# Seven of nine conditioning vectors summed on VectorE instead of made on TensorE

## The chip, the core and the metric

The kernel runs on one core of a Trainium2 chip. A core has five engines with one instruction queue each: PE (TensorE, matrix products into PSUM), DVE (VectorE), ACT (ScalarE), POOL (GpSimd) and SP, whose queue here issues nearly all DMAs. Every queue is worked off in order. The metric is the device time of the whole program in microseconds (us), the median of several runs.

## The reference

One layer of a diffusion backbone, in float32, on 1024 latent tokens and 128 context tokens: a feed-forward block with half weight, a token mixer (attention beside a gated recurrence), a second feed-forward block, a final norm. What matters here is how the conditioning enters:

```
mod_p = (silu(c_ctx) @ w_ada + b_ada).reshape(9, 1024)   # context tokens
mod_s = (silu(c)     @ w_ada + b_ada).reshape(9, 1024)   # latent tokens
x = x + 0.5 * m[2] * swiglu(modulate(x, g[0], m[0], m[1]), w1, w3, w2)
x = x + m[5] * token_mixer(modulate(x, g[1], m[3], m[4]), ...)
x = x + 0.5 * m[8] * swiglu(modulate(x, g[2], m[6], m[7]), w1', w3', w2')
# modulate(x, g, shift, scale) = rmsnorm(x, g) * (1 + scale) + shift
```

So there are nine vectors of 1024 numbers, each for two conditions, m[0] to m[8], and each is a product of a 1024-vector with a 1024x1024 slice of `w_ada` (4 MB). A gate m[2] is first needed when the first feed-forward block's results are added to x, m[3] and m[4] at the first norm behind that block, m[5] behind the mixer, m[6] and m[7] at the norm after that, m[8] at the end.

## The kernel before, in words

Activations are kept with features on the 128 partitions and all 1152 tokens along the free dimension, so x is eight tiles of 128x1152. Every float32 product is made of three TensorE products of split operands (high x high, low x high, high x low, `mm3`), which is why nearly every operand is first split: ACT writes the high part, POOL or DVE subtracts it to get the low part.

A feed-forward block (`ffn_fast`, called with l=0 and l=1) has three parts:

- **Plain blocks.** The first `PLAIN` = 4 (l=0) or 3 (l=1) of 22 hidden blocks, eight products of 128x288 per hidden block.
- **Half products.** The other 18 (19) hidden blocks in a scheme that makes seven products of half depth instead of eight (`fast_block`, L1484; its weights come from `fast_ops`, L1449). Per hidden block there are seven steps n; in each step PE makes one half product for two column pairs, each of 12 matmuls of 128x288 into one PSUM bank. DVE reads the bank out into `et` (L1507 to L1521), makes the low part of the next weights (`wo`, L1479), and POOL makes sums of weight pieces (L1474).
- **The way down.** The hidden activations come back from DRAM two hidden blocks at a time (`hr`, L1573), are split by ACT and POOL (L1579, L1580), as are their weights (L238, L239). `down_group` (L451) then goes over eight feature blocks m and three column chunks; one chunk (a tick) is six matmuls into a PSUM bank called `dn` (three of them), and DVE adds the bank, times the gate, to x (L442). Nine such groups per block for l=0, then `down_last`.

**The nine vectors** are made by `ada_pe` (L247): eight row blocks of 512 KB are loaded, and for each PE makes four small float32 matmuls with the SiLU of both conditions as 32-column weights; ACT, two transposes and one DVE instruction finish a vector, `ada_end` scales it. m[1] and m[0] are made at the start, m[2] beside the first plain blocks (L1533), and m[3] to m[8] on the way down of l=0 (L1616): `self.bg` is advanced on every fourth tick.

**What sets the order.** The program's order of calls is a priority. A scheduler places each engine's instructions in its queue beforehand, and an instruction of lower priority is pulled ahead where the scheduler finds the engine free, so the calls of a background generator such as `bg` don't stand where they are called. Buffers come from rings (`half` six, `wide` eight, `slim` four, `tt` 25 tiles); a tile that is reused waits for its last reader.

Of the kernel before, what the change touches and what calls it, by code (L numbers as in the profile page):

```python
# [9 lines left out]
F32 = mybir.dt.float32  # L10
F32R = mybir.dt.float32r
BF16 = mybir.dt.bfloat16
U8 = mybir.dt.uint8
AF = mybir.ActivationFunctionType
ALU = mybir.AluOpType
# [4 lines left out]
P = 128  # L20
D = 1024
KT = D // P
# [40 lines left out]
def rows(w, m):  # L63

    return w[m // 4][:, ts(m % 4, P)] if isinstance(w, list) else w[:, 0, ts(m, P)]
# [12 lines left out]
def weave(gens):  # L78
    gens = list(gens)
    while gens:  # L80
        for g in list(gens):
            try:
                yield next(g)
            except StopIteration:
                gens.remove(g)


class Trunk:
# [158 lines left out]
    def ada_pe(self, m, buf):  # L247
# [26 lines left out]
        )  # L274
        self.ada_end(m)

    def ada_end(self, m):
        nc = self.nc
        if m in (2, 8):
            nc.vector.tensor_scalar(self.modt[:, m], self.modt[:, m], 0.5, None, ALU.mult)  # L280
        if m % 3 == 1:
            nc.vector.scalar_tensor_tensor(
                self.gs[:, m // 3],
                self.modt[:, m],
                1.0,
                self.ng[:, m // 3].unsqueeze(2).to_broadcast([P, KT, 2]),
                ALU.add,
                ALU.mult,
            )
# [161 lines left out]
    def down_group(self, w2, fs, hs, gm, ws=None):  # L451
        ws = ws or [self.load_w(w2[f], 1, D) for f in fs]
        for m in range(KT):
            for c in self.chunks:
                self.down([(rows(wh, m), rows(wl, m)) for wh, wl in ws], hs, gm, c, m)
                self.ticks += 1
                if self.ticks % 4 == 0:
                    next(self.bg, None)

    def down_last(self, w2, fs, hs, gm, nxt):  # L460
# [1064 lines left out]
    def ffn_fast(self, l, gm, nxt):  # L1525

        nc = self.nc
        w2 = self.a["w2"][l]
        plain = PLAIN[l]
        self.hs = self.dp.tile([NF, P, T], F32, name=f"hs{l}")  # L1530
        self.puts, self.ticks = [], 0
        sums, ops, made = iter(()), iter(()), []
        steps = iter(()) if l else weave([self.whole(), self.ada_pe(2, lambda k: self.wide("wada"))])  # L1533
        for f in range(plain):
            ws = self.pre[f] if l == 0 and f < 2 else [self.load_w(self.a["w13"][l, f, j], KT, P) for j in range(2)]
            if f == 2 - l:
                for _ in steps if l == 0 else self.tail:
                    pass
                sums = self.sums()
            if f == plain - 1:  # L1540
                ops = self.fast_ops(l, range(plain, NF))
            n = 0

            def after():
                nonlocal n
                if l and f == 0:
                    next(self.tail, None)
                elif f < 2 - l:
                    next(steps, None)
                else:  # L1550
                    next(sums, None)
                if f == plain - 1 and n > 7 and n % 2:
                    made.append(next(ops))
                n += 1

            self.plain_block(l, f, ws, after)
        for _ in sums:
            pass
        made = [w for w in made if w]
        self.B = None  # L1560
        pend, ws, raws = [], [], []
        tile = partial(self.tt, F32) if l == 0 else self.wide
        split = partial(self.wide, dt=F32R) if l == 0 else partial(self.tt, F32R)
        spare = partial(self.tt, F32R) if l == 0 else partial(self.wide, dt=F32R)

        def load_x(k):
            t = self.tt(F32, f"x{k}")
            nc.sync.dma_start(t[:, :T], self.xs[k] if l else self.a["xT"][k])
            return t

        def load_h(f):
            raw = tile("hr")[:, :T]
            nc.sync.dma_start(raw, self.hs[f])  # L1573
            return f, raw

        def split_h(f, raw):
            new = partial(self.tt, F32R) if f in (16, 17) else split
            hh, hl = new(name="hh")[:, :T], new(name="hl")[:, :T]
            nc.scalar.copy(hh, raw)  # L1579
            nc.gpsimd.tensor_sub(hl, raw, hh)  # L1580
            return f, (hh, hl)

        def load_w2(f):
            return self.load_w(w2[f], 1, D, home=spare if f % 2 else None)

        for f in range(plain, NF):
            blocks = [self.fast_block(f, r) for r in range(2)]
            for g in blocks:
                next(g)
            for n in range(7):  # L1590
                if len(made) < 6:
                    w = next(ops, None)
                    if w:
                        made.append(w)
                w = made.pop(0)
                for t in self.puts:
                    self.put(*t)
                self.puts = []
                for g in blocks:
                    g.send(w)  # L1600
                if f == NF - 1:
                    if n == 2:
                        raws = [load_h(0), load_h(1)]
                    elif n == 3:
                        ws.append(load_w2(0))
                        pend.append(split_h(*raws[0]))
                    elif n == 4:
                        pend.append(split_h(*raws[1]))
                    elif n == 5:
                        ws.append(load_w2(1))  # L1610
                        self.x = [load_x(0), load_x(1)]
        for t in self.puts:
            self.put(*t)
        self.x += [load_x(k) for k in range(2, KT)]
        if l == 0:
            self.bg = chain(*[self.ada_pe(m, lambda k: self.tt(F32, "wada")) for m in range(3, 9)])  # L1616
        for f in range(2, NF):
            pend.append(split_h(*load_h(f)))
            if f % 2 and f < NF - 1:
                fs, hs = zip(*pend[:2])  # L1620
                self.down_group(w2, fs, hs, gm, ws or [load_w2(v) for v in fs])
                pend, ws = pend[2:], None
        for _ in self.bg:
            pass
        fs, hs = zip(*pend)
        self.down_last(w2, fs, hs, gm, nxt)


def layout(inp):
    import numpy as np  # L1630

    f = lambda n: np.asarray(inp[n])
# [4 lines left out]
    a = {}  # L1637
# [14 lines left out]
        1,  # L1652
    )
    a["w_ada"] = f("w_ada")[0]
    a["w13"] = np.stack(
        [np.stack([tiles(f(f"ffn{l}_w1")[0]), tiles(f(f"ffn{l}_w3")[0])], 1) for l in (1, 2)]
    )
# [2 lines left out]
    o = np.cumsum([0, 384, 256, 32, 512, 512, 512, 512, 512, 1024, 1024])  # L1660
    qc, kvc, kr, hq, hff, hfb, hi, hgt, ga, gr = [wi[:, o[i] : o[i + 1]] for i in range(10)]
    sl = lambda w, i, n: w[:, i * n : (i + 1) * n]
    ws = []
# [83 lines left out]
```

## Time and profile before

| | us |
|---|---|
| median of 3 runs | 3035.35 (3032.83 to 3035.94) |
| the profiled execution | 3036.94 |
| its span | 3035.2 |
| PE busy | 2928.8 (96%) |
| DVE busy | 1897.1 (63%) |
| POOL busy | 1031.6 (34%) |

The span is the time from the first to the last instruction of the profiled execution. In time, the start and plain blocks of l=0 end at about 160 us, its half products run to about 562, its way down to about 860, the mixer follows, and the second feed-forward block with its own half products and way down ends the program. PE is busy in nearly every slice; DVE is busy for a good half of most.

### The profile page before, as it was taken

The numbers are of one execution on the slowest core, as the hardware profiler recorded it, in microseconds if no ns is written. First come the engines' busy times: TensorE is split into PE (matmuls) and PEld (weight loads), VectorE is DVE, ScalarE is ACT, GpSimd is POOL, SyncE is SP. The second block draws the span as 40 slices with busy tenths as digits, with TensorE's granted clock in tenths as the row PEclk, the third lists the DMA queues.
The fourth block names the chain that finished last, engine by engine and source line by source line (L and its number), as shares of the span: only waits on it lengthen the run. The fifth ranks groups of instructions, "written<-read, shape, count | busy, mean of one in ns | idle before, by whom it ended". The sixth has DMA issues, their size and how long they took to land. (4 is left out here: it accounts for less than half of the span.)

```text
span 3035.2 us, 49626 instructions
## 1 busy us (share of the span) xinstructions
PE 2928.8 (96%) x18960; PEld 2747.1 (91%) x18960; DVE 1897.1 (63%) x3751; ACT 1234.9 (41%) x2370; POOL 1031.6 (34%) x831
## 2 busy tenths in 40 slices
PE   7999999999999999999999999989999999999998
PEld 5899999988888988888998778779989999999997
DVE  7665455455568777787636677765674555546665
ACT  5432232211165464645434677741262222332113
POOL 3122222434233333332325444533242222226324
PEclk9999999999999999999999999999999999999999
DMA  6632222754221111111110000143352222226211
GB/s 244 228 100 77 72 74 73 299 188 174 84 94 46 43 43 47 38 45 45 59 62 20 11 17 21 52 146 104 101 187 74 74 73 77 77 95 220 89 44 63
DMA packets 141678, 279.25 MB, mean 92 GB/s; under 512 B 18112, under 2 KB 82560, under 8 KB 141440
## 3 DMA queue, kind: packets, MB, share of 16 engines
q1 hardware_dynamic: 141296, 275.75, 26.8%
q8 instruction: 150, 2.46, 0.3%
q14 instruction: 88, 0.72, 0.1%
q10 hardware_dynamic: 144, 0.33, 0.0%
HBM read 212.49 MB, written 63.52 MB: 91 GB/s over the span
## 5 line engine op out<-in xcount | busy, mean ns | idle before, releaser
L442 DVE SCALAR_TENSOR_TENSOR x<-dn,modt,x 128x256 f32<-128x256 f32 (+4 forms) x728 | 353.5, 506 | 237.1 <-PE dn L415 236.5
L1503 PE MATMUL b<-xo,wo 128*128 128x288 f32 x3552 | 484.3, 295 | 0.0
L1503 PEld LDWEIGHTS b<-xo,wo 128*128 128x128 f32 x3552 | 476.2, 188 | 0.0
L413 PE MATMUL mm<-xh,wh 128*128 128x384 f32 (+1 forms) x1008 | 361.9, 359 | 5.4 <-DVE q L610 3.2
L1503 PE MATMUL b<-bh,wo 128*128 128x288 f32 x1776 | 365.7, 295 | 0.0
L239 POOL TENSOR_TENSOR wl<-raw,wh 128x1024 fp32r<-128x1024 f32 (+1 forms) x106 | 235.8, 2226 | 380.7 <-ACT wh L238 378.1
L415 PE MATMUL mm<-xh,wl 128*128 128x384 f32 (+1 forms) x1008 | 342.6, 340 | 2.0 <-POOL wl L239 1.8
L414 PE MATMUL mm<-xl,wh 128*128 128x384 f32 (+1 forms) x1008 | 342.2, 339 | 0.0
L1503 PEld LDWEIGHTS b<-bh,wo 128*128 128x128 f32 x1776 | 288.7, 188 | 0.0
L1503 PE MATMUL b<-bl,wo 128*128 128x288 f32 x888 | 261.4, 294 | 0.0
L1478 ACT CAST wo<-raw 128x512 fp32r<-128x512 f32 x185 | 114.8, 621 | 256.3 <-PE b L1503 155.9
L238 ACT CAST wh<-raw 128x1024 fp32r<-128x1024 f32 (+1 forms) x108 | 104.3, 967 | 254.2 <-PE dn L414 142.3
L413 PEld LDWEIGHTS mm<-xh,wh 128*128 128x128 f32 (+1 forms) x1008 | 190.9, 189 | 15.3 <-DVE q L610 4.0
L413 PE MATMUL dn<-hh,wh 128*128 128x384 f32 (+2 forms) x576 | 201.2, 349 | 2.4 <-DVE x L442 1.2
L1479 DVE TENSOR_TENSOR wo<-raw,wo 128x512 fp32r<-128x512 f32 x185 | 128.7, 697 | 117.0 <-ACT wo L1478 116.4
L415 PE MATMUL dn<-hh,wl 128*128 128x384 f32 (+2 forms) x576 | 194.6, 338 | 1.0 <-POOL wl L239 1.0
L414 PE MATMUL dn<-hl,wh 128*128 128x384 f32 (+2 forms) x576 | 194.0, 337 | 0.0
L415 PEld LDWEIGHTS mm<-xh,wl 128*128 128x128 f32 (+1 forms) x1008 | 190.6, 189 | 3.6 <-POOL wl L239 2.1
L414 PEld LDWEIGHTS mm<-xl,wh 128*128 128x128 f32 (+1 forms) x1008 | 191.0, 189 | 1.7 <-issue 0.4
L1580 POOL TENSOR_TENSOR hl<-hr,hh 128x1152 fp32r<-128x1152 f32 x44 | 117.8, 2686 | 193.2 <-PE dn L414 87.6
L1237 POOL TENSOR_TENSOR ehl<-e,ehl 128x512 fp32r<-128x512 f32 x93 | 122.4, 1321 | 142.0 <-ACT ehl L1235 79.0
L1503 PEld LDWEIGHTS b<-bl,wo 128*128 128x128 f32 x888 | 167.3, 188 | 0.0
(379 smaller groups left out, 6996.3 us busy)
## 6 DMA issues: line engine op xcount, KB each, us to landing
raw<-in_w SPq DMA_DIRECT2D x148, 256.0 KB, 3.0
wada<-in_w_ada SPq DMA_DIRECT2D x72, 512.0 KB, 5.8
raw<-in_w SPq DMA_DIRECT2D x58, 512.0 KB, 3.8
hr<-hs SPq DMA_DIRECT2D x44, 576.0 KB, 4.8
hs<-et SPq DMA_DIRECT2D x148, 144.0 KB, 1.7
raw<-in_w_in SPq DMA_DIRECT2D x41, 512.0 KB, 3.6
hb<-hd SPq DMA_DIRECT2D x44, 288.0 KB, 3.3
x<-in_xT SPq DMA_DIRECT2D x16, 576.0 KB, 8.7
```

What stands on the lines that cost most here:

```text
L238: pin(self.nc.scalar.copy(wh, raw))
L239: pin((eng or self.nc.gpsimd).tensor_sub(wl, raw, wh))
L413: nc.tensor.matmul(ps, wh, xh, start=start and i == 0, stop=False)
L414: nc.tensor.matmul(ps, wh, xl, start=False, stop=False)
L415: nc.tensor.matmul(ps, wl, xh, start=False, stop=stop and i == n - 1)
L442: nc.vector.scalar_tensor_tensor(self.x[m][:, a:b], ps[:, a - lo : b - lo], self.modt[:, gm, m, s : s + 1], self.x[m][:, a:b], ALU.mult, A ...
L1237: eng.tensor_sub(el, e, eh)
L1478: nc.scalar.copy(wh, src[i])
L1479: nc.vector.tensor_sub(wl, src[i], wh)
L1503: nc.tensor.matmul(ps, w[:, k], x[:, k, :QW], start=first, stop=last, skip_group_check=home != i)
L1580: nc.gpsimd.tensor_sub(hl, raw, hh)
```

## The change

Only m[0] and m[1] are still made by `ada_pe`. A new generator, `ada_sum`, makes the others on DVE. `w_ada` is given a second time, transposed, so that output features lie on partitions and the 1024 inputs along the free dimension, in two halves of 512. A unit is one vector, one output block of 128 and one half: its weights (256 KB) are loaded into one half of a `wada` tile, so two loads can be there at a time, and two DVE instructions, one per condition, multiply them with the SiLU of the condition (broadcast to all partitions, `cb`) and write the sum over the 512 into one column of `adac`; the product itself goes to `junk`. A vector is 16 units. m[2] to m[5] (64 units) go beside the half products of l=0, m[6] and m[7] (32 units) on the way down of l=0, m[8] (16 units) beside the half products of l=1. On the way down the background is advanced on every third tick now.

```diff
+    def ada_sum(self, ms, cb, w2, small, fine=False):
+        nc, a = self.nc, self.a
+        HD = D // 2
+        acc = small("adac")[:, : 32 * len(ms)].rearrange("p (m h k s) -> p m h k s", m=len(ms), h=2, k=KT)
+        junk = small("junk").bitcast(BF16)[:, :HD]
+        w2 = w2("wada")
+        ws = [w2[:, :HD], w2[:, HD : 2 * HD]]
+        units = [(h, i, k) for h in range(2) for i in range(len(ms)) for k in range(KT)]
+        def load(n):
+            h, i, k = units[n]
+            nc.sync.dma_start(ws[n % 2], a["w_aT"][ms[i] - 2, k, :, ts(h, HD)])
...
+        for n, (h, i, k) in enumerate(units):
+            if not i and not k:
+                cs = [cb("cb")[:, :HD] for _ in range(2)]
...
+                for s in range(2):
+                    nc.scalar.activation(cs[s], cs[s], AF.Silu)
+                yield
+            if n + 1 < len(units):
+                load(n + 1)
+            for s in range(2):
+                o = acc[:, i, h, k, s : s + 1]
+                nc.vector.scalar_tensor_tensor(junk, ws[n % 2], 1.0, cs[s], ALU.mult, ALU.mult, accum_out=o)
+                if fine and not s:
+                    yield
+            if h and k == KT - 1:
+                nc.vector.tensor_add(acc[:, i, 0], acc[:, i, 0], acc[:, i, 1])
+                b = self.bada[:, ms[i]].unsqueeze(2).to_broadcast([P, KT, 2])
+                nc.vector.tensor_tensor(self.modt[:, ms[i]], acc[:, i, 0], b, ALU.add)
+                self.ada_end(ms[i])
+            yield
...
-                if self.ticks % 4 == 0:
+                if self.ticks % 3 == 0:
                     next(self.bg, None)
...
-        steps = iter(()) if l else weave([self.whole(), self.ada_pe(2, lambda k: self.wide("wada"))])
+        steps = iter(()) if l else self.whole()
...
+        ada = self.ada_sum((8,) if l else (2, 3, 4, 5), self.half, partial(self.tt, F32), self.slim)
...
+                if (n in (1, 4)) if l else (7 * f + n) % 3:
+                    next(ada, None)
...
-            self.bg = chain(*[self.ada_pe(m, lambda k: self.tt(F32, "wada")) for m in range(3, 9)])
+            new = partial(self.tt, F32)
+            self.bg = self.ada_sum((6, 7), new, new, self.slim, True)
```

How the queues change is seen at three places. First DVE in the half products of l=0, from the second product of a hidden block on, before: the bank reads into `et` and the low weight parts `wo`.

```order
L1507 TENSOR_TENSOR et<-b_2295,et 128x288
L1507 TENSOR_TENSOR et<-b_2309,et 128x288
L1479 TENSOR_TENSOR wo<-raw,wo 128x512
L1509 TENSOR_TENSOR et<-b_2326,et 128x288
L1509 TENSOR_TENSOR et<-b_2340,et 128x288
L1479 TENSOR_TENSOR wo<-ws,wo 128x512
L1511 TENSOR_TENSOR et<-b_2361,et 128x288
```

The same place in the changed kernel (lines are 39 higher), where `junk,adac` is a sum of a unit:

```order
L1546 TENSOR_TENSOR et<-b_2029,et 128x288
L306 SCALAR_TENSOR_TENSOR junk,adac<-wada,cb 128x512 x2
L1546 TENSOR_TENSOR et<-b_2043,et 128x288
L1518 TENSOR_TENSOR wo<-raw,wo 128x512
L306 SCALAR_TENSOR_TENSOR junk,adac<-wada,cb 128x512
L1548 TENSOR_TENSOR et<-b_2060,et 128x288
L306 SCALAR_TENSOR_TENSOR junk,adac<-wada,cb 128x512
L1548 TENSOR_TENSOR et<-b_2074,et 128x288
L1518 TENSOR_TENSOR wo<-ws,wo 128x512
L306 SCALAR_TENSOR_TENSOR junk,adac<-wada,cb 128x512
L1550 TENSOR_TENSOR et<-b_2098,et 128x288
L306 SCALAR_TENSOR_TENSOR junk,adac<-wada,cb 128x512 x2
```

The scheduler pulled the sums together: 17 stand in one hidden block, nearly twice what the calls would spread, so each half of the 64 units fills about four hidden blocks without a gap, and the others have none.

Then DVE on the way down of l=0, two feature blocks m, before:

```order
L442 SCALAR_TENSOR_TENSOR x_5986<-dn,modt,x_5986 128x256
L442 SCALAR_TENSOR_TENSOR x_5986<-dn,modt,x_5986 128x128
L442 SCALAR_TENSOR_TENSOR x_5986<-dn,modt,x_5986 128x384 x2
L442 SCALAR_TENSOR_TENSOR x_5988<-dn,modt,x_5988 128x256
L442 SCALAR_TENSOR_TENSOR x_5988<-dn,modt,x_5988 128x128
L442 SCALAR_TENSOR_TENSOR x_5988<-dn,modt,x_5988 128x384 x2
```

and in the changed kernel:

```order
L481 SCALAR_TENSOR_TENSOR x_6147<-dn,modt,x_6147 128x256
L481 SCALAR_TENSOR_TENSOR x_6147<-dn,modt,x_6147 128x128
L306 SCALAR_TENSOR_TENSOR junk,adac<-wada,cb 128x512
L481 SCALAR_TENSOR_TENSOR x_6147<-dn,modt,x_6147 128x384
L306 SCALAR_TENSOR_TENSOR junk,adac<-wada,cb 128x512
L481 SCALAR_TENSOR_TENSOR x_6147<-dn,modt,x_6147 128x384
L481 SCALAR_TENSOR_TENSOR x_6149<-dn,modt,x_6149 128x256
```

Two sums stand in each feature block, through 33 feature blocks, a little over four of the nine groups.

Last SP's queue at the start of the way down in the changed kernel (before, `wada` loads of 128x1024 stood there in sixes):

```order
L1613 DMA hr<-hs_631 128x1152 x2
L289 DMA wada<-in_w_aT 128x512
L244 DMA raw<-in_w 128x1024
L289 DMA wada<-in_w_aT 128x512
L244 DMA raw<-in_w 128x1024
L1613 DMA hr<-hs_631 128x1152
L289 DMA wada<-in_w_aT 128x512
```

Each unit's load now stands between loads of activations (`hr`) and weights (`raw`), which wait for buffers.

## Rows read from the trace of the kernel before

**Rows 1.** The page's first part: busy us, share, instructions.
```profile
PE 2928.8 (96%) x18960; PEld 2747.1 (91%) x18960; DVE 1897.1 (63%) x3751; ACT 1234.9 (41%) x2370; POOL 1031.6 (34%) x831
```

**Rows 2.** Stretches: start:end, length, each engine's busy us, clock, DMA share, GB/s.
```profile
80.00:160.00 80.00, 76.75 (x585) 73.26 (x585) 56.54 (x120) 37.42 (x73) 12.05 (x6) 0.98 0.67 220
200.00:240.00 40.00, 40.00 (x304) 40.00 (x303) 20.69 (x39) 11.58 (x23) 10.13 (x8) 1.00 0.22 73
560.00:600.00 40.00, 39.20 (x254) 34.20 (x253) 22.61 (x46) 7.41 (x8) 15.42 (x7) 1.00 1.00 390
600.00:640.00 40.00, 40.00 (x260) 34.66 (x259) 21.08 (x44) 6.38 (x7) 16.18 (x7) 1.00 0.66 243
```

**Rows 3.** PE's waits between 80 and 160 us: total us, times, longest.
```profile
PE adap L254 <- DMA wada<-in_w_ada: 2.8, 2, 1.4
PE adat L268 <- ACT adar L265: 0.5, 1, 0.5
```

**Rows 4.** PE in time on the way down: start, us, instruction, count.
```profile
642.57 0.33 PE L414 MATMUL dn<-hl,wxh 128*128 128x384 f32 x1
642.74 0.34 PE L415 MATMUL dn<-hh,wxl 128*128 128x384 f32 x1
643.01 0.64 PE L254 MATMUL adap<-wada,sc 128*32 128x256 f32 x8
643.58 0.45 PE L413 MATMUL dn<-hh,wh 128*128 128x384 f32 x1
643.87 0.33 PE L414 MATMUL dn<-hl,wh 128*128 128x384 f32 x1
...
647.70 0.34 PE L415 MATMUL dn<-hh,wxl 128*128 128x384 f32 x1
647.88 0.38 PE L268 MATMUL adat<-ident,adar 128*128 128x128 f32 x2
648.01 0.42 PE L413 MATMUL dn<-hh,wh 128*128 128x384 f32 x1
648.27 0.33 PE L414 MATMUL dn<-hl,wh 128*128 128x384 f32 x1
```

**Rows 5.** DVE in time at the start of the way down.
```profile
565.33 1.79 DVE L442 SCALAR_TENSOR_TENSOR x<-dn,modt,x 128x256 f32<-128x256 f32 x4
```

**Rows 6.** DVE instructions by form: out<-in, count, busy us, mean ns.
```profile
L317 DVE SCALAR_TENSOR_TENSOR rs<-rt,rs 128x512 f32<-128x512 f32 x1 | 0.7, 677 | 0.0
L316 DVE SCALAR_TENSOR_TENSOR rt<-rt,rs 128x512 f32<-128x512 f32 x1 | 1.2, 1249 | 0.0
L442 DVE SCALAR_TENSOR_TENSOR x<-dn,modt,x 128x384 f32<-128x384 f32 x304 | 187.6, 618 | 133.1 <-PE dn L415 133.0
L442 DVE SCALAR_TENSOR_TENSOR x<-dn,modt,x 128x256 f32<-128x256 f32 x152 | 73.6, 484 | 78.1 <-PE dn L415 78.0
L442 DVE SCALAR_TENSOR_TENSOR x<-dn,modt,x 128x128 f32<-128x128 f32 x176 | 60.3, 343 | 0.0
```

**Rows 7.** ACT's instructions of line 1252, the only sum with its elementwise result.
```profile
L1252 ACT ACTIVATION_READ_ACCUMULATOR pc<-sps,nm x8: 189/198/203, 1713.5 to 1997.9; 128x1 f32 x8
```

**Rows 8.** DVE and POOL in time where the second half products end.
```profile
2730.08 5.33 POOL L1580 TENSOR_TENSOR hl<-hr,hh 128x1152 fp32r<-128x1152 f32 x2
2732.32 0.46 DVE L1515 TENSOR_TENSOR et<-b,et 128x288 f32<-128x288 f32 x1 [4.31 <-PE b L1503]
2732.88 2.84 DVE L1516 TENSOR_TENSOR et<-et 128x288 f32<-128x288 f32 x1
2735.36 2.61 POOL L239 TENSOR_TENSOR wl<-raw,wh 128x1024 fp32r<-128x1024 f32 x1
2735.64 0.45 DVE L1515 TENSOR_TENSOR et<-b,et 128x288 f32<-128x288 f32 x1
2736.19 2.10 DVE L1516 TENSOR_TENSOR et<-et 128x288 f32<-128x288 f32 x1
```

**Rows 9.** POOL by form, the first row between 200 and 500 us, the others 600:760.
```profile
L1474 POOL TENSOR_TENSOR raw<-raw,ws 128x512 f32<-128x512 f32 x14 | 18.1, 1289 | 126.4 <-issue 126.4
...
L1580 POOL TENSOR_TENSOR hl<-hr,hh 128x1152 fp32r<-128x1152 f32 x13 | 34.8, 2681 | 39.2 <-PE adap L254 26.7 <-PE dn L414 6.4 <-ACT hh L1579 6.1
L239 POOL TENSOR_TENSOR wl<-raw,wh 128x1024 fp32r<-128x1024 f32 x6 | 14.4, 2399 | 0.0
```

**Rows 10.** Loads: KB each, median us to landing, the page's first, then 535 to 610 us.
```profile
raw<-in_w SPq DMA_DIRECT2D x148, 256.0 KB, 3.0
...
wada<-in_w_ada SPq DMA_DIRECT2D x18, 512.0 KB, 10.3
hr<-hs SPq DMA_DIRECT2D x10, 576.0 KB, 8.6
```

More of the change, by code (lines that the diff above doesn't have):

```diff
@@ L275, in ada_pe @@
         self.ada_end(m)
+    def ada_sum(self, ms, cb, w2, small, fine=False):
[9 more added lines that the diff above has]
+            nc.sync.dma_start(ws[n % 2], a["w_aT"][ms[i] - 2, k, :, ts(h, HD)])
+        cs = None
+        for n, (h, i, k) in enumerate(units):
+            if not i and not k:
+                cs = [cb("cb")[:, :HD] for _ in range(2)]
+                for s in range(2):
+                    nc.sync.dma_start(cs[s], a["cr"][s : s + 1, ts(h, HD)].to_broadcast([P, HD]))
+                if not n:
+                    load(0)
+                for s in range(2):
[3 more added lines that the diff above has]
+                load(n + 1)
+            for s in range(2):
+                o = acc[:, i, h, k, s : s + 1]
[8 more added lines that the diff above has]
+            yield
     def ada_end(self, m):
@@ L1611, in ffn_fast @@
                         self.x = [load_x(0), load_x(1)]
+        assert next(ada, 1) == 1
         for t in self.puts:
@@ L1654, in layout @@
     a["w_ada"] = f("w_ada")[0]
+    a["w_aT"] = f("w_ada")[0][:, 2 * D :].T.reshape(7, KT, P, D)
+    a["cr"] = np.concatenate([f("c"), f("c_ctx")[None]])
     a["w13"] = np.stack(
```

## Prediction

> **What bounds the kernel now.** I read the page first, then the busy time by stretches, then the time lines of the two stages that the change touches. PE is busy for 96% of the span [rows 1], and in the half products and on the way down for practically all of it, at full clock [rows 2]. So every microsecond of PE work that goes is a microsecond of the span, as long as nothing else comes last. DVE is the engine that takes the work over. It is busy for 20.69 of 40 us in the half products and 21.08 of 40 on the way down [rows 2], so the reader is to ask not whether it has room on average, but whether it has room where the scheduler has put the new sums.
>
> **What goes.** On the way down, one row block of a vector sits between two ticks. The matmul starting at 642.74 and the second after it, at 643.87, are 1.13 us apart; two such matmuls without it take 2 x 0.175 (642.57 to 642.74 shows the pitch) = 0.35. One row block thus costs PE 0.78 us [rows 4]. Six vectors of eight: 48 x 0.78 = 37.4. The two transposes cost 648.27 - 647.70 - 0.35 = 0.22 each time [rows 4], six times 1.3. Together 38.7 us. The third vector, beside the plain blocks, is eight row blocks at the same price, 6.2, and 0.2 for its transposes; PE also waited 2.8 us for its weights and 0.5 for ACT [rows 3]. PE is idle there for 3.25 us of 80 [rows 2], so these waits are all there is. Gain 6.4 to 9.7; I take 9.3. **Removed from PE: 48 us.**
>
> **What a sum costs on DVE.** 224 sums of 512 columns are added. A DVE instruction of that form without a sum, both inputs in SBUF, takes 677 ns where nothing disturbs it, 1249 where something does [rows 6]. Back to back the next one starts earlier: four bank reads whose own durations add to 618 + 618 + 484 + 343 = 2063 ns [rows 6] take 1.79 us together [rows 5], 0.09 less per pair. So 0.60 us without the sum. That the sum has a price of its own is seen on ACT alone, where the accumulator is read by an extra instruction of 198 ns [rows 7]; DVE has no such row, so 0 to 0.20, below nothing being excluded because one output more is written. I take 0.10: 0.70 us, with 0.60 and 0.80 as ends.
>
> **What POOL does to it.** DVE instructions with two SBUF inputs wait for a POOL instruction that runs: the product of two `et` tiles, 458 ns as a rule, takes 2.84 and 2.10 us, and both times ends when POOL's split does, while the bank read between them, with one input in PSUM, keeps its 0.45 [rows 8]. The wait is 1.6 to 2.4 us. The new sums have two SBUF inputs; the bank reads on the way down do not. Behind a blocked sum stand the bank reads, and behind those PE, which has three banks and can go on for about two ticks (2.1 us) less a read of 0.62, so some 1.4 us once.
>
> **The way down.** A feature block is 18 matmuls, 18 x 0.175 = 3.14 us of PE. DVE needs 1.79 less the overlap at its end, 1.73, for the four bank reads, and now 2 x 0.70 for sums: 3.13. It is exactly full, with no room for the port. Per group POOL makes four splits of 2.4 to 2.7 us [rows 9] (25 of them in 160 us, the `wxl` ones having the `wl` row's time); the 33 feature blocks are 4.1 groups, so 17 splits. A bank read of about 0.6 fits beside a split before the next sum stands at the port, so I take 1.7 per split, near the lower of the two waits seen: 29 us, less 1 for the banks. **Lost: 28 us.** With the sum at 0.60 and no blocking it is nothing (33 x (2.93 - 3.14) is room); with 0.80 and 2.4 per split 33 x 0.19 + 41 = 47. Nothing below zero: PE's work in these ticks doesn't shrink further.
>
> **The half products of l=0.** A hidden block is 168 matmuls, 22.1 us at 304 in 40 [rows 2]; DVE's share is 20.69/40 x 22.1 = 11.4. There are 17 sums in it where they stand densest: 11.9, and 0.7 because a pair in a row waits for its own first result and loses the overlap. POOL's four sums of weights take 1.29 each [rows 9]; at 0.6 per one that is 2.5. Total 26.5, so DVE falls behind by 4.4 per hidden block, over 64/17 = 3.8 of them 16.7. PE does not feel the first 7: a bank that DVE must have read is written again five half products later, 5 x 12 x 0.132 = 7.9, less a read of 0.46 and a hop. So about 9.5 us per stretch, and there are two (one for each half of the 512s): **lost 19 us.** The ends: nothing, if a sum is 0.60 and POOL's price stays out (1.5 x 3.8 is under 7); 54, with 0.80, 1.1 per POOL instruction and a wait for loads of 1 us per hidden block. In l=1 the 32 sums stand in two stretches of one hidden block each, 4.4 under 7, so nothing (4 at the far end). The twelve small loads of the conditions and ACT's twelve SiLUs lie beside idle ACT (11.58 of 40 busy [rows 2]).
>
> **The sum.** -48 + 28 + 19 = -1 us on the profiled execution of 3036.94 (span 3035.2 and 1.7 around it). That execution is 1.6 above the median of the runs, so I forecast 3034: what PE gives up comes back as banks that DVE reads late.
>
> **Rivals.**
> (A) DVE keeps up. If the splits fall beside bank reads rather than sums, and the accumulator costs nothing, losses are some 18 us (10 on the way down, 8 in the half products): 3035 - 30 = 3005. For it: 47% of DVE's time is free on average [rows 2]. Against: the order has the sums packed, two in each feature block.
> (B) The loads come late. Each unit's load may be issued only when the sums two units back are done, and in DVE's queue about 3.7 us of work (four reads and two to three sums) stands between them and the sums that need it. 256 KB land in 3.0 us in the median, but between 535 and 610 us, when the DMA engines are full (share 1.00 from 560 to 600 [rows 2]), loads twice as big took 8.6 to 10.3 [rows 10]. Half of that is 4.3 to 5.2, and SP's queue puts `raw` and `hr` loads that wait for buffers in front. From 3.7 on each such load holds DVE, and all bank reads behind it: the 12 units of the first 50 us at 2.5 us each are 30. 3034 + 30 = 3064, slower. Against: the 9 MB of early `wada` loads that filled the engines there are gone.
> (C) A sum runs at half rate. DVE's bank reads cost (618 - 343)/256 = 1.07 ns per column [rows 6]; at two cycles a sum costs 512 x 1.07 = 0.55 us more. That is 1.1 x 33 = 36 on the way down, 64 x 0.55 = 35 in each of two stretches, and 17 x 0.55 + 4.4 - 7 = 6.7 in each of two of l=1: 119 more, 3153. Against: the plain form with both inputs in SBUF runs at full rate, 677 ns for 512 [rows 6]. The Trainium skill states this rule (Vector Engine (DVE) Microarchitecture Reference, section "Points that are easy to get wrong"): a scalar-tensor-tensor with two non-bf16 SBUF sources runs at half throughput, as no read port is left for the accumulator. The rows here disagree for the form without a sum; with a sum no run here shows it.
>
> **How the numbers follow.** A difference of up to 0.2%, 6 us, is about what a measurement of this kernel can't tell from none. Forecast (losses 33 to 62, 3020 to 3049): 0.42, of which 0.14 faster, 0.19 same, 0.09 slower. A 0.25, faster. B 0.22, slower. C 0.11, slower. So faster 0.39, same 0.19, slower 0.42. The range from 3000 to 3078 holds the forecast, nearly all of A and B, and leaves out C and the far ends of A and B, 0.2; the forecast's own is 3020 to 3049.
>
> **What will show it.** `junk` rows of 0.65 to 0.8 us mean undisturbed, with maxima near 3 us on the way down beside POOL's splits; PE waits for DVE's `x` there of 20 us and more, where it had almost none; PE waits for `et` only in two stretches of the half products; no `adap` after 60 us. Wrong would be: sums over 1.1 us where POOL is idle (C), DVE waiting for `wada` loads by tens of us (B), PE as dense as before with DVE at 90% (A).

## The result, and the profile after

The changed kernel takes 3040.36 us (median; 3036.58 to 3045.84) where the kernel before takes 3035.39 beside it: ratio 1.0017, interval 1.0010 to 1.0024. The forecast was 3034. The time lies in the range, but the sign is the other one: 1 us was to be gained and 5 were lost. The profiled execution has a span of 3037.4 us (before 3035.2), so the stages below account for 2.2 of the 5; the rest is that the profiled execution of the changed kernel lies 1.2 us under its median (3039.14) and that of the kernel before 1.55 over its own.

I cut the span at the first matmul of a stage (time line of PE, the tiles `b`, `dn` and `nps`; the last is the norm that follows the way down). Times in us:

| stage | before | after | difference | forecast |
|---|---|---|---|---|
| start and plain blocks of l=0 | 161.0 | 154.5 | -6.5 | -9.3 |
| half products of l=0 | 401.7 | 422.3 | +20.6 | +19 |
| way down of l=0 | 289.5 | 282.0 | -7.5 | -38.7 + 28 = -10.7 |
| mixer and plain blocks of l=1 | 1460.8 | 1457.6 | -3.2 | 0 |
| half products of l=1 | 423.9 | 423.0 | -0.9 | 0 |
| rest | 298.3 | 298.0 | -0.3 | 0 |

The engines' busy time in the page of the changed kernel: PE is busy 32.6 us less than before [rows 1], though the span didn't fall.

```profile
PE 2896.2 (95%) x18498; PEld 2743.2 (90%) x18498; DVE 2070.8 (68%) x4206; ACT 1233.2 (41%) x2375; POOL 1049.2 (35%) x831
```

The stretches of [rows 2] in the changed kernel (start:end, length, busy us of each engine, granted clock, DMA share, GB/s):

```profile
80.00:160.00 80.00, 80.00 (x594) 80.00 (x594) 60.43 (x128) 36.22 (x72) 18.57 (x7) 0.98 0.60 189
200.00:240.00 40.00, 36.63 (x268) 35.58 (x268) 38.22 (x91) 9.02 (x22) 7.15 (x5) 0.99 0.49 156
560.00:600.00 40.00, 37.21 (x233) 36.62 (x232) 23.09 (x44) 10.34 (x13) 17.64 (x7) 0.96 0.76 279
600.00:640.00 40.00, 34.55 (x190) 32.41 (x189) 38.54 (x78) 9.81 (x10) 20.30 (x8) 1.00 0.67 233
```

Beside the plain blocks PE has no gap from 80 us on; one of 3.3 us lies just ahead of that, from 76.4 to 79.7, and comes up again below. In the half products and on the way down PE was the engine without a gap and DVE was busy for half of the time; now DVE has 38.2 and 38.5 of 40 us and PE loses 3.4 and 5.5. What PE waits for, first in the half products (155 to 576 us), then on the way down (577 to 858; total us, times, longest); before, PE waited for nothing in the first of these stages and 2.4 us in the second:

```profile
PE b L1542 <- DVE et L1548: 9.6, 8, 2.4
PE b L1542 <- DVE et L1550: 3.2, 4, 1.7
```
```profile
PE dn L452 <- DVE x L481: 20.3, 19, 2.6
```

The sums on the way down, and DVE's reads of the accumulator after each (duration min/median/max in ns, first and last start):

```profile
L306 DVE SCALAR_TENSOR_TENSOR junk<-wada,cb x64: 673/680/3143, 592.6 to 723.5; 128x512 bf16<-128x512 f32 x64
L306 DVE DVE_READ_ACCUMULATOR junk<-wada,cb x64: 73/77/84, 595.3 to 726.3; 128x1 f32 x64
```

So a sum lasts 0.68 us as a rule, the read behind it 0.08, and a sum up to 3.1 at the worst. (What the two take of DVE's time is less than their total, as rows further down show.) One such case in time, from the lines of DVE, POOL and PE at the start of the way down, with the stretches beside it:

```profile
591.17 0.48 DVE L481 SCALAR_TENSOR_TENSOR x<-dn,modt,x 128x256 f32<-128x256 f32 x1 [0.44 <-PE dn L454]
592.57 2.82 DVE L306 SCALAR_TENSOR_TENSOR junk<-wada,cb 128x512 bf16<-128x512 f32 x1 [0.91 <-DMA wada<-in_w_aT]
595.32 0.08 DVE L306 DVE_READ_ACCUMULATOR junk<-wada,cb 128x1 f32 x1
595.32 0.34 DVE L481 SCALAR_TENSOR_TENSOR x<-dn,modt,x 128x128 f32<-128x128 f32 x1
```
```profile
589.55 5.29 POOL L1620 TENSOR_TENSOR hl<-hr,hh 128x1152 fp32r<-128x1152 f32 x2 [13.97 <-ACT hh L1619]
```
```profile
595.81 0.41 PE L452 MATMUL dn<-hh,wh 128*128 128x384 f32 x1 [2.56 <-DVE x L481]
```
```profile
592.00:594.00 2.00, 1.25 (x8) 0.92 (x6) 1.44 (x1) 0.43 (x1) 2.00 (x2) 1.00 0.93 368
594.00:596.00 2.00, 0.19 (x1) 0.22 (x2) 2.00 (x4) 0.00 (x0) 0.84 (x1) 1.00 0.24 97
596.00:598.00 2.00, 2.00 (x9) 2.00 (x9) 2.00 (x7) 0.00 (x0) 0.00 (x0) 0.61 0.29 99
598.00:600.00 2.00, 2.00 (x8) 2.00 (x7) 1.72 (x5) 0.00 (x0) 0.00 (x0) 0.53 1.07 308
600.00:602.00 2.00, 2.00 (x14) 2.00 (x13) 1.32 (x5) 1.05 (x1) 0.48 (x1) 1.00 0.77 250
```

The reader is to follow one chain. The sum starts at 592.57 while POOL's second split runs until 594.84, and ends 0.55 us after it, so it did its own work only then. The bank read behind it starts at 595.32, and PE goes on at 595.81, after standing for 2.56 us. From then on its granted clock is near 0.5 (the lower of its two levels, 1.2 GHz) for most of 4 us: 8 or 9 matmuls in 2 us instead of 14. No term of the forecast had this second part. It is seen at two more places on the way down, behind waits of 1.97 and 1.95 us, and at two in the half products, behind 2.35 and 1.78 (the eighth entry is the clock):

```profile
651.00:655.00 4.00, 4.00 (x14) 4.00 (x15) 2.94 (x9) 0.00 (x0) 0.00 (x0) 0.57 0.85 266
712.00:716.00 4.00, 3.52 (x11) 3.56 (x12) 4.00 (x9) 1.13 (x1) 2.17 (x1) 0.57 0.49 163
197.00:201.00 4.00, 3.62 (x17) 3.29 (x16) 2.55 (x6) 2.42 (x6) 2.17 (x2) 0.57 0.05 19
251.00:256.00 5.00, 4.93 (x27) 4.61 (x26) 4.93 (x13) 2.26 (x5) 0.22 (x1) 0.66 0.32 98
```

### The profile page after: what moved, and what is told of

Same layout as the page of the kernel before. It is cut to its first block, busy times and chain, and to the rows that moved or that the text cites. A ratio compares the mean times of both kernels' runs of the same rounds, so it can differ in the third digit from the quotient of the medians.

```text
span 3037.4 us, 49240 instructions
## 1 busy us (share of the span) xinstructions
PE 2896.2 (95%) x18498; PEld 2743.2 (90%) x18498; DVE 2070.8 (68%) x4206; ACT 1233.2 (41%) x2375; POOL 1049.2 (35%) x831
## 3 DMA queue, kind: packets, MB, share of 16 engines
q8 instruction: 146, 2.39, 0.3%
## 5 line engine op out<-in xcount | busy, mean ns | idle before, releaser
L306 DVE SCALAR_TENSOR_TENSOR junk<-wada,cb 128x512 bf16<-128x512 f32 x224 | 205.9, 919 | 16.9 <-DMA wada<-in_w_aT 14.5
```

Source lines behind the costliest of these rows:

```text
L306: nc.vector.scalar_tensor_tensor(junk, ws[n % 2], 1.0, cs[s], ALU.mult, ALU.mult, accum_out=o)
```

## The experiments

Fourteen kernels. All edits are against the changed kernel, and all diffs are cut to their core. A stage's time comes from one profiled execution; where the code of a stage is the same, it varies: the way down takes 280.9 to 283.5 us in the five kernels that leave it as in the changed one (changed, e4, e6, e7, e7b), the half products 421.5 to 422.3 in three (changed, e2, e3). The stages and times:

| kernel | half products l=0 | way down l=0 | median | ratio to before (interval) |
|---|---|---|---|---|
| before | 401.7 | 289.5 | 3035.39 | |
| changed | 422.3 | 282.0 | 3040.36 | 1.0017 (1.0010 to 1.0024) |
| e4_half_in_order | 401.6 | 280.9 | 3023.15 | 0.9954 (0.9937 to 0.9970) |
| e7_no_pool_half | 401.8 | 280.9 | 3021.57 | 0.9944 (0.9930 to 0.9959) |
| e7b_pool_unread | 420.8 | 282.9 | 3039.29 | 1.0014 (1.0003 to 1.0025) |
| e6_one_condition | 413.6 | 283.5 | 3032.36 | 0.9991 (0.9982 to 1.0001) |
| e8_four_halves | 417.4 | 280.4 | 3036.10 | 1.0004 (0.9995 to 1.0013) |
| e6c_one_four_halves | 419.8 | 280.1 | 3039.16 | 1.0012 (1.0000 to 1.0023) |
| e1_half_on_pe | 401.7 | 308.3 | 3052.16 | 1.0060 (1.0045 to 1.0075) |
| e2_way_down_on_pe | 421.5 | 270.2 | 3031.24 | 0.9986 (0.9976 to 0.9995) |
| e3_psum_way_down | 421.6 | 261.0 | 3025.55 | 0.9961 (0.9948 to 0.9974) |
| e10_all_in_order | 401.7 | 266.3 | 3007.34 | 0.9910 (0.9893 to 0.9926) |
| e5_both | 401.6 | 261.2 | 3002.53 | 0.9885 (0.9871 to 0.9900) |
| e9_psum_four_halves | 401.6 | 257.1 | 2996.66 | 0.9867 (0.9853 to 0.9882) |
| e11_in_order_psum_four | 402.0 | 254.2 | 2994.06 | 0.9860 (0.9845 to 0.9875) |
| e5b_in_order_psum | 401.7 | 251.5 | 2993.66 | 0.9857 (0.9843 to 0.9872) |

My theory was that DVE is overfull where the scheduler has packed the sums, mainly because sums with two SBUF inputs stand behind POOL's instructions, and that PE then waits for banks read late. The rivals: late loads of weights; DVE's work by itself; another effect of the new arrangement.

**Where the losses sit.** Each half of the change is undone alone.

```diff
 # e1: vector 2 on PE beside the plain blocks, 3 to 5 on PE on the way down
-        steps = iter(()) if l else self.whole()
+        steps = iter(()) if l else weave([self.whole(), self.ada_pe(2, ...)])
-        ada = self.ada_sum((8,) if l else (2, 3, 4, 5), ...)
+        ada = self.ada_sum((8,), ...) if l else iter(())
-            self.bg = self.ada_sum((6, 7), new, new, self.slim, True)
+            self.bg = chain(*[self.ada_pe(m, ...) for m in (3, 4, 5)], self.ada_sum((6, 7), ...))
-                if self.ticks % 3 == 0:
+                if self.ticks % 2 == 0:
 # e2: vectors 6 and 7 on PE on the way down
-            self.bg = self.ada_sum((6, 7), new, new, self.slim, True)
+            self.bg = chain(*[self.ada_pe(m, ...) for m in (6, 7)])
```

> Vectors 2 to 5 go back to PE: the first of them beside the plain blocks as before, three on the way down (a step at every second tick), where 6 and 7 then still are summed on DVE. Theory: the half products of l=0 are back at 401.6 us; the plain blocks and what is ahead of them at about 161; the way down, with 24 row blocks more on PE (24 x 0.78 = 19) and fewer feature blocks in which sums stand, 282 + 19 = 301 or some us under it. Rival (the half products' 20.7 us come from something else in the changed kernel, such as a new arrangement of tiles): the stage stays over 415.

> Vectors 6 and 7 go back to PE on the way down (16 row blocks and two times two transposes), the others stay on DVE. Theory: the half products keep 422.3 us; the way down loses the 31 us of waits and gains 16 x 0.78 + 0.4 = 13 of PE: about 264 instead of 282.0; total about 3022. Rival (the way down is longer for another reason than the sums): it takes 290 or more.

In e1 the half products are back at 401.7 to the tenth, and in e2 they keep their loss (421.5): that loss belongs to the sums that stand there, with their loads. The way down took 308.3 in e1 and 270.2 in e2, 7 and 6 over what I expected. Both have one long wait that the changed kernel doesn't have, for a split of weights by POOL: 4.8 us in e1, and in e2 (576 to 845 us)

```profile
PE dn L454 <- POOL wxl L239: 4.3, 1, 4.3
```

Behind it PE's granted clock in e2 is 0.50 from 616 to 619, an estimated 3 x 0.5 = 1.5 us more, so that the two nearly make up e2's 6. In e1 the sums also stand at every second tick and not every third.

**The half products: place, port, loads, number.**

```diff
 # e4: in program order beside the half products
+                t = nc.vector.scalar_tensor_tensor(junk, ...)
+                if not fine:
+                    self.tc.keep_in_program_order(t)
 # e7: POOL's sums of weights left out, the products get other tiles
-            src = {1: a11, 6: s2, 7: a21, 5: s1, 2: a12, 4: a22, 3: a12}
+            src = {1: a11, 6: s2 if l else a11, 7: a21, 5: s1 if l else a21, 2: a12, 4: a22, 3: a12}
-                for o, x, y, op in pre.get(i, ()):
+                for o, x, y, op in pre.get(i, ()) if l else ():
 # e7b: src as in e7; POOL computes the sums, nobody reads them
-                7: ((a21, a11, a21, ALU.subtract),),
+                7: ((a21 if l else s1, a11, a21, ALU.subtract),),
-                3: ((a12, a12, s2, ALU.subtract),),
+                3: ((a12 if l else s1, a12, s2, ALU.subtract),),
 # e6: one condition
-            for s in range(2):
+            for s in range(1 if len(ms) == 4 else 2):
 # e8 (and e6c = e6 + e8): four halves of weights on the way
-            if n + 1 < len(units):
-                load(n + 1)
+            if n + 3 < len(units):
+                load(n + 3)
```

> The sums beside the half products are held in the order in which the program calls them, some 9 per hidden block and not 17; nothing else is changed. Theory (DVE is overfull where 17 sums stand in one hidden block): the half products of l=0 take 401.6 us as before or up to 405 instead of 422.3, the way down keeps its 282.0, and the total is about 3021. Rival 1 (each sum costs by its loads, which come late): the same number of loads, so the stage stays within 5 us of 422.3. Rival 2 (the stage grew because DVE works more at all, wherever the sums stand): over 415 us.

> POOL's sums of weights in the half products of l=0 are left out (products that need them take another tile, so what is computed is not the reference's); the sums of DVE stay at 17 per hidden block. Theory (DVE falls behind because sums stand blocked behind POOL): most of the 20.7 us of this stage goes, 402 to 408 us. Rival (DVE is overfull by its own 17 sums without POOL): by the terms of the forecast 11.4 + 12.6 = 24.0 us of DVE in 22.1 of PE, some 7 us per stretch, which the banks hide in part; with that the stage stays at 410 or more. Late loads: no change, 422.

In both the whole 20.6 us are gone (401.6 and 401.8), and PE waits for nothing in the stage. PE and the other engines in e4's half products, as a stretch:

```profile
156.00:557.00 401.00, 401.00 (x3022) 401.00 (x3021) 290.21 (x647) 121.55 (x240) 109.69 (x74) 1.00 0.40 130
```

The same 128 sums, with POOL as busy as ever, and no microsecond of PE is lost. Counted in stretches of 22 us, 8 to 11 sums start in each in e4, 13 to 17 in the changed kernel, and 17 to 19 in e7. So 18 sums in one hidden block fit when POOL is silent: DVE's own work does not overfill it, and the rival by which it does (410 us or more) is out. But e7 also takes away something else: products no longer wait for POOL's sums. Hence the next kernel.

> As the kernel without POOL's sums of weights beside the half products of l=0 (401.8 us there), but POOL computes the same four sums per hidden block, of the same inputs and size, and nobody reads them, so no product waits for them (what is computed is not the reference's). It keeps POOL's use of the port and takes out the chain from POOL over ACT and DVE to the products. Theory (the sums wait at the port): the stage is back over 412 us. Rival (DVE was late because weights came late through POOL): it stays at 402 to 405.

420.8: with POOL at work and nobody waiting for its results the loss is back, 19.1 of 20.6. PE's waits there (155 to 575 us), all of them banks that DVE reads late:

```profile
PE b L1542 <- DVE et L1550: 12.0, 11, 1.6
PE b L1542 <- DVE et L1548: 3.2, 3, 1.9
```

Between e7 and e7b only POOL's instructions differ, and the 128 sums are busy for 105.9 us instead of 88.1. So POOL's use of the port is enough, without anybody waiting for its results, where 13 to 17 sums stand in a hidden block.

> In the half products of l=0 only the first of the two conditions is summed (the second is left at zero, so what is computed is not the reference's): half of DVE's sums, all of the loads, at the same places. Theory (DVE overfull): 8 to 9 sums per hidden block leave DVE room, and the stage takes 401.6 to 405 us. Rival (late loads, 256 KB each, which hold DVE and the bank reads behind it): the loads are the same, the stage stays within 5 us of 422.3.

> Four halves of weights instead of two are on the way at a time, in both stages. Theory (DVE overfull; it waits for weights for 14.5 us in all, 4.3 to 6 in each stretch of the half products): at most 10 us back in the half products, 1 or 2 on the way down, total 3028 to 3040. Rival (late loads): most of the 20.7 and of the 31 goes, total under 3015.

> Beside the half products of l=0 one condition of the two is summed (the other is left at zero, not the reference's result), and four halves of weights are on the way instead of two. With one condition and two halves the stage took 413.6 us, DVE waiting 28.6 for weights; with both conditions and four halves 417.4. Theory (DVE falls behind by sums, port and waits for loads together): with half of the sums and no waits for loads it keeps up, 401.6 to 405 us. Rival (loads were not what was left; the port alone is): within 4 us of 413.6.

These three say what does not settle it. e6 halves DVE's sums (10 to 12 in 22 us) and the stage still loses 11.9 us: my expectation of 405 fell, and so did the rival's of 422. DVE waits there for weights for 28.6 us (10.3 in the changed kernel). e8 takes the changed kernel's 10.3 away (0.2 us left) and gives back 4.9: these waits are a quarter of the loss. I then expected that e6c, with both, would lose nothing; it loses 18.1, and so the rival, within 4 us of 413.6, fell too. With four halves the scheduler puts 13 to 16 sums of one condition into 22 us, as many as it had of two, and DVE still waits for weights there, 11.4 us in all. PE's waits in e6c (155 to 575):

```profile
PE b L1546 <- ACT et L1556: 7.6, 5, 2.5
PE b L1546 <- DVE et L1552: 3.5, 3, 2.1
```

Two thirds of them are now for ACT, whose instruction stands behind a cast that waits for POOL's sums of weights: between 196 and 201 us POOL had waited 11.0 us for its `raw` load, and ACT 8.9 for POOL. So there seems to be a second way to the same loss, over late `raw` loads, POOL and ACT. e7b shows that it isn't needed; how much of the 20.6 us of the changed kernel goes by it stays open.

**The way down: port and density.**

```diff
 # e3: SiLU conditions into two PSUM banks, so a sum has one SBUF input
+                if fine:
+                    ps = [self.bank("up", "cbp", HD) for _ in range(2)]
-                    nc.scalar.activation(cs[s], cs[s], AF.Silu)
+                    nc.scalar.activation(ps[s] if fine else cs[s], cs[s], AF.Silu)
+                if fine:
+                    cs = ps
 # e10: every sum in program order
+                self.tc.keep_in_program_order(nc.vector.scalar_tensor_tensor(junk, ...))
 # e5 = e3 + e4; e5b = e3 + e10; e9 = e5 + e8; e11 = e5b + e8
```

> On the way down the SiLU conditions are written to two PSUM banks that are free there, so that each sum has one input in SBUF and one in PSUM; the number and place of the sums are as in the changed kernel. Theory (31 us of the way down are lost to DVE sums that wait for POOL's splits): the way down takes 251 to 255 us instead of 282.0, the half products keep 422.3, the total is about 3010, and no sum on the way down takes over 1.2 us. Rival 1 (DVE is full by its own work, 3.13 of 3.14 us per feature block, and POOL is incidental): over 272 us. Rival 2 (the loads of weights come late): within 4 us of 282.

The way down takes 261.0 us, 21.0 less, but not the 251 to 255 that I expected, and the total is 15 over what I wrote. No sum waits any more (longest 690 ns), and PE's waits fall from 20.3 us to 6.2:

```profile
L310 DVE SCALAR_TENSOR_TENSOR junk<-wada,cbp x64: 673/678/690, 593.0 to 708.8; 128x512 bf16<-128x512 f32 x64
L310 DVE DVE_READ_ACCUMULATOR junk<-wada,cbp x64: 76/83/86, 593.6 to 709.4; 128x1 f32 x64
```
```profile
PE dn L456 <- DVE x L485: 6.2, 6, 3.5
```

The port is the larger part, as the theory says; but 10.2 us over the 250.8 of PE's own work stayed.

> Both edits together: the conditions of the way down in PSUM, and the sums beside the half products held in program order. If the two losses are separate and each is what the theory says, half products of about 402 to 405 us and a way down of 251 to 255, and a total of about 2990. If a third thing (late loads, DVE's total work) sets both, the total stays over 3025.

261.2 and 401.6: the two losses add up without touching each other. The total of 3002.5 is 12 over what I wrote, 10 of them those just named.

> All sums are held in the order in which the program calls them; nothing else differs from the changed kernel. Beside the half products that is what has already been run alone (stage 401.6 us). On the way down the 64 sums now stand among 247 bank reads instead of 130, one per feature block and not two, and keep both inputs in SBUF. Theory (the loss needs both POOL's port and a DVE that is full): per feature block 1.73 + 0.76 = 2.5 us of 3.14, so the 0.65 us left in each of 62 blocks, 40 us, nearly takes the 31 splits x 1.7 us = 53: way down 251 to 264 us instead of 280.9, total 2987 to 3003. Rival (the port's waits cost PE wherever the sums stand): 31 x 1.4 us and more, way down 280 or over.

266.3, two us over what I expected, with the port's waits still there (sums up to 3.0 us) and PE's waits at 12.2 us instead of 20.3:

```profile
L307 DVE SCALAR_TENSOR_TENSOR junk<-wada,cb x64: 674/682/3016, 572.6 to 781.6; 128x512 bf16<-128x512 f32 x64
```
```profile
PE dn L454 <- DVE x L483: 7.8, 9, 1.6
PE dn L454 <- DVE modt L314: 4.4, 2, 3.0
```

So a stop of 3 us seems to cost PE only what the free time of the neighbouring feature blocks doesn't hold. One sum per block gives 15.7 us back, against 21.0 for the free port.

> Half products' sums in program order, the way down's conditions in PSUM with its two sums per feature block, and four halves of weights on the way instead of two. In the same kernel with two halves the way down took 261.2 us, DVE waited 7.7 us there for weights in 8 waits and PE 6.9 for bank reads. Theory (late loads are the smaller part: one wait of DVE for weights stands before one of PE's five, and 3.5 us of PE's come from small instructions of DVE behind POOL): 256 to 259. Rival (loads are what is left): 251 to 254. Rival (DVE full by its own work, 1.73 + 2 x 0.76 = 3.25 of 3.14 us): 260 to 262.

257.1, as the theory had it: late loads are 4 of the 10 us. What is left is not the sums. Here are the small instructions at the end of a vector in e9, and POOL beside them:

```profile
688.79 0.63 DVE L317 TENSOR_TENSOR adac<-adac 128x16 f32<-128x16 f32 x1
689.45 2.31 DVE L319 TENSOR_TENSOR modt<-adac,vec 128x16 f32<-128x16 f32 x1
691.80 2.53 DVE L328 SCALAR_TENSOR_TENSOR gs<-modt,vec 128x16 f32<-128x16 f32 x1
694.25 1.78 DVE L488 SCALAR_TENSOR_TENSOR x<-dn,modt,x 128x384 f32<-128x384 f32 x4
```
```profile
686.70 2.69 POOL L1627 TENSOR_TENSOR hl<-hr,hh 128x1152 fp32r<-128x1152 f32 x1 [0.96 <-ACT hh L1626]
689.35 2.39 POOL L239 TENSOR_TENSOR wl<-raw,wh 128x1024 fp32r<-128x1024 f32 x1
691.69 2.61 POOL L1627 TENSOR_TENSOR hl<-hr,hh 128x1152 fp32r<-128x1152 f32 x1
```

Two instructions of 16 columns, 0.16 us each in other kernels, take 2.31 and 2.53 because each ends with a split, and PE waits 3.5 us once behind them.

> All sums in program order, and the way down's conditions in PSUM. Theory: the way down has neither the port nor the fullness and costs what PE costs, 289.5 - 38.7 = 250.8, at most 254; total 2988 to 2993. Rival (what is left after both edits, 10 us over 250.8 in the kernel with conditions in PSUM alone, is another cost, such as late loads of weights): 257 to 261.

> All three: every sum in program order, conditions of the way down in PSUM, four halves on the way. Theory: with one sum per feature block loads have 6.3 us from issue to use even with two halves, so four bring nothing over the kernel without them: way down 250.8 to 254, total 2988 to 2993. Rival (loads still hold DVE): 3 us or more under that kernel.

251.5 us in e5b, which is the 250.8 that the forecast's removal term gives when nothing is lost; four halves (e11, 254.2) bring nothing more, as expected. PE's waits in e5b's way down, and the stretch:

```profile
PE dn L460 <- POOL wl L239: 1.0, 1, 1.0
PE dn L458 <- DVE x L487: 0.4, 1, 0.4
```
```profile
558.00:809.00 251.00, 249.56 (x1415) 248.12 (x1415) 189.09 (x451) 50.01 (x56) 98.79 (x40) 1.00 0.44 148
```

e5b is the best version: 2993.66 us, 1.4% faster than the kernel before (e11's total can't be told from it). The same sums on the same engine, placed one per feature block and kept off POOL's port, turn a small loss into a gain of 42 us.

## Why the prediction had the wrong sign

**PE's removal: right.** 38.7 us on the way down: e5b gives 289.5 - 251.5 = 38.0.

**The plain blocks: 9.3 forecast, 6.5 measured.** The waits for `wada` and ACT are gone. But PE now comes to its first plain products sooner and waits once for DVE, a wait that the kernel before doesn't have (60 to 100 us):

```profile
PE ps L452 <- DVE hf L1478: 3.3, 1, 3.3
```

DVE was making `hx`, 1.35 us a piece, at that time. e1, with that vector back on PE, doesn't have this wait and takes 160.5 us up to its half products; the other kernels, without it, have the wait (3.3 to 4.4 us) and take 154.1 to 155.8. The forecast took the waits that go as gained and did not ask what PE would wait for next at that place.

**A sum: 0.70 us forecast, 0.60 measured on the way down.** The sum's 0.68 us overlaps with what follows, and the read of the accumulator costs no place of its own: in e3 the bank read behind a sum starts with that read, 0.60 us after the sum.

```profile
613.08 0.68 DVE L310 SCALAR_TENSOR_TENSOR junk<-wada,cbp 128x512 bf16<-128x512 f32 x1
613.68 0.08 DVE L310 DVE_READ_ACCUMULATOR junk<-wada,cbp 128x1 f32 x1
613.68 0.61 DVE L485 SCALAR_TENSOR_TENSOR x<-dn,modt,x 128x384 f32<-128x384 f32 x1
```

That is the median of the 59 sums of e3's way down that stand before a bank read. Where another sum follows, in the half products, it is 0.72. So 0.60, the forecast's lower end, was right on the way down, and the 0.10 for the accumulator was not there. Rival C is out: no sum runs at half rate. The Trainium skill's rule (Vector Engine (DVE) Microarchitecture Reference, "Points that are easy to get wrong") doesn't hold here: two f32 inputs in SBUF and the accumulator take 680 ns for 512 columns, as without the sum [rows 6]. Rival A, a DVE that keeps up, is what e5b is, and needs two edits for it. **Rival B** is small: e8 shows 4.9 us for the half products and 1.6 for the way down (within what that stage varies by), e9 4.1 for the way down with the port free, where 30 were put.

**The way down: 28 us forecast, 31.2 measured** (282.0 - 250.8), near it by luck. With the sum at 0.60 a feature block needs 1.73 + 1.20 = 2.93 of DVE in 3.14 of PE, so DVE was not "exactly full". The forecast's own working then gives 17 x 1.7 = 29 for the port, less 33 x 0.21 = 7 of room, less 1 for the banks: an estimate of 21, and e3, which frees the port, gave 21.0 back. The other 10.2 are losses for which this term had nothing: 4.1 go with the late loads (e9), and in what e9 keeps, PE waits 4.5 us for bank reads, 3.5 of them behind the two small instructions at a vector's end, and 1.6 for POOL's splits of weights. A sum too dear by 0.10 and the parts left out nearly cancelled. Neither loss stands for itself: with one sum per feature block (e10) the port costs 15.5, and with neither the port nor the second sum (e5b) 0.7 is left. The Trainium skill says of the port pair that DVE and GpSimd (here POOL) share (SBUF — State Buffer, "Who interferes with whom") that it is an exclusive lock, for which a DVE instruction with two SBUF inputs contends with a GpSimd instruction that reads SBUF, and one with at most one SBUF input, outside the 2-port modes, does not. The rows here agree: the longest sum on the way down falls from 3143 to 690 ns when one input is in PSUM (e3). One reading of the forecast is a little off: in [rows 8] DVE's products end some 0.3 us behind POOL's splits, and not with them.

**The half products: 19 us forecast, 20.6 measured, and in e7 and e7b the working held.** Without POOL the forecast's terms give 26.5 - 2.5 = 24.0 us of DVE in 22.1 of PE, 1.9 per hidden block and 7.2 in 3.8 of them, which the 7 us that the banks hide take up; e7 lost nothing. With POOL they give 19; e7b lost 19.1. What the working could not have foreseen is e6 and e6c: by it half of the sums lose nothing, and they lost 11.9 and 18.1. So it lacks a part that seems to go by the loads and by POOL and ACT, and whose share in the 20.6 stays open.

**The step that failed is the sum, -48 + 28 + 19 = -1,** and in it two terms. Of the 48 that PE gives up, the plain blocks' 9.3 took every wait there as gained: 6.5 came, because PE met a wait of 3.3 us for DVE. And the 28 of the way down were 31.2, because late loads and the ends of the vectors were put at nothing. With 1.6 more in the half products the misses are 2.8 + 3.2 + 1.6 = 7.6 us, all on one side. The other stages gave 4.4 back, 3.2 of it in the mixer (kernels whose code is the same there lie between 1457.4 and 1460.9, so that is no effect that can be shown). That makes +2.2 where -1 was forecast. Each of the first two misses alone turns the sign.

**A part that no term had is the clock.** PE's idle time on the way down is 22.9 us (281.0 - 258.08), less than the 28; but its busy time is 258.08 us, where e5b needs 249.56 for about as many matmuls. In the half products it is 13.7 idle, and 407.29 busy instead of 401.00. Of these 8.5 and 6.3 us the five stretches at a lower clock explain about 5 and 3.3 (busy time, times the part of the clock that is missing: 4.00 x 0.43 twice and 3.52 x 0.43; 3.62 x 0.43 and 4.93 x 0.34); the clock was 1.00 in both stages in [rows 2]. What of it lengthens a stage is not shown: DVE was busy for most of these stretches, so a faster PE might have waited for it instead, and no experiment took the clock alone away.

## What to carry to other kernels

Before work is moved to an engine that is half idle on average, look where a scheduler will put it: here the same 128 sums cost 20.6 us at 13 to 17 in 22 us and nothing at 8 to 11. An elementwise instruction with two inputs in SBUF can wait a whole POOL instruction, however small it is itself; one input in PSUM frees it. A forecast that is a small difference of large terms has no sign: ask of each wait that goes what the engine meets next, and of each loss what else stands in the same queue.

## What the runs showed that I had not expected

- Behind five waits of PE, of 1.78 to 2.56 us, the granted clock was 0.57 to 0.66 over the next 4 or 5 us; after the first, some 4.00 x 0.43 = 1.7 us more of PE's time. Not every stall has this: behind one of 1.64 us, which ends at 608.7, the clock stayed at 1.00.
- DVE has an instruction of its own for the accumulator, 77 to 83 ns, like ACT's of 198 [rows 7], but cheaper, and a bank read behind a sum starts together with it.
- A 128x16 addition on DVE takes 0.16 us, and 2.31 beside a POOL split of 2.39.
